# C11, the fourth and the sixth product: PSUM banks handed on by ScalarE's copies in place of VectorE's adds

## The chip, the cores and the metric

The kernel runs on one core of a Trainium2 chip. The metric is the time of an execution on the device in microseconds (us); the time of a kernel is the median of its runs.

## The reference

```
a, b: 4096 x 4096, float32, normally distributed; alpha = 0.01
x = a @ b
out = where(x > 0, x, alpha * x)        # float32
```

## The kernel before

The matrix product is done in 16-bit floats with 32-bit sums in PSUM, as a Strassen-Winograd scheme. The output is cut into 4 row groups `g` and 4 column groups `j` of 1024 each. The block (0, 0) is done plainly at the start (L283). The other 15 are "regions", done in the order (0,1) (0,2) (0,3), (1,2) (1,0) (1,3) (1,1), (2,2) (2,0) (2,3) (2,1), (3,2) (3,0) (3,1) (3,3).

A region's a and b are each cut into four blocks (A11 to A22, B11 to B22). Seven products take the place of eight; `product(n, ...)` (L808, its matmul at L819) does one as 64 matmuls, each of 128 x 128 weights on 128 x 512, into four PSUM banks. TensorE's order through a region is product 0 (A11 on B11), 1 (A12 on B21), 2, the fourth, 4, the sixth and the seventh; numbers count from 0 and ordinals from one, so "the fourth" is product 3. Some of these are cut once more in the same way: the fourth, the sixth and the seventh of most regions with g > 0, and the fifth of region (2,3) alone. Such a product is seven `quarter_product`s (L762) of 16 matmuls each, on 128 x 256.

The kinds of region: `first_of_group` (column 2), `turning` (the last of a group when the next group's A is loaded and transposed meanwhile: (0,3), (1,1), (2,1)), `in_quarters` (g > 0 and not turning), `in_fourth` (in_quarters and not the first of its group), `in_fifth` ((2,3)).

The eight PSUM banks are two sets of four, `y` and `z`; the sets change places from region to region. In the old kernel product 0 fills `y`, product 1 fills `z`, product 2 goes on in `y`, the fourth takes `z` again, product 4 goes on in `y`, the sixth takes `z`. What leaves the banks goes by two engines:

- ScalarE: `keep` (L829) copies four banks to tiles `c` in SBUF (L832), and the copies inside the quartered products.
- VectorE: `add` (L1041) adds four banks to tiles of SBUF, one instruction to each; in the quartered products it adds single banks (`more` in the sixth, the loop over `parts` for the fourth at L1219).

VectorE forms as well the sums of B's blocks (`b_sum`, L592) and of their quarters (L686 to L696, called `t3_of_b`, `sums_of_b`), the sums of A's, the leaky product at the end (L313), and the transposes of A. Quarter sums of A that come again (`kept_qs`, `kept_qa`) are stored in DRAM and loaded back (`load_sums`, L754).

Two things run beside the products and are ordered by hand. Measures (`measure(i, half, nt)`, begin and end) have ScalarE square a block of b (L231) and VectorE reduce the squares (L240 to L264); `EARLY` says which stand behind product 0 of which region (for (2,0): B12 and then B21), and `late_ones`, `middle` name other places. ScalarE also squares the rows of a (L611).

Loads: b comes through GpSimd's queue, which converts to 16 bit (`fetch_unit`, L536: pieces of 512 KB, two to a tile, so a pair of issues is one tile). `fetch_b(i + 1, ...)` puts the next region's tiles where tiles of the same block are now, so each pair waits for the last matmul that reads the tile it overwrites. In region (2,0) the four pairs for (2,3) are, in order, two that overwrite the block of B that the fourth reads and two that overwrite the block that product 4 reads; the last two are what product 0 of (2,3) reads. SyncE issues the stores of the output (L1054) and other loads; ScalarE issues a few.

The whole order is a schedule written out by hand (`manual_schedule`): each engine does its instructions in the order of the program.

Of the kernel before, what the change touches and what calls it, by code (L numbers as in the profile page):

```python
# [31 lines left out]
MT = 4  # L32
# [16 lines left out]
def kernel(  # L49
# [17 lines left out]
    nc = tc.nc  # L67
# [725 lines left out]
    for i, (g, j) in enumerate(regions):  # L793
# [14 lines left out]
        def product(n, banks, first):  # L808
            name, half, nt = PRODUCTS[n]

            ks_here = (0, 1) if n == 0 and second_of_group else ks
            todo = [(k, c) for k in ks_here for c in range(KC)]
            order = [(mt, k, c) for k, c in todo for mt in range(MT)]
            if n == 0 and late_s2:

                order = [(mt, k, c) for k in ks_here for mts in ((0, 1), (2, 3)) for c in range(KC) for mt in mts]
            for mt, k, c in order:
                t = operand(g, name, k)
                nc.tensor.matmul(  # L819
                    banks[mt], a_cols(t, c, mt, t is first_a), B(half, nt, k)[:, c, :],  # L820
                    start=first and (k, c) == todo[0], stop=(k, c) == todo[-1], skip_group_check=not first,
                )
# [12 lines left out]
        def fourth_in_quarters(banks, tq, sx):  # L835
# [11 lines left out]
            if not turning:  # L847
                quarter_product(sx[4], b[1, 1], into(other), True)
# [7 lines left out]
            if turning:  # L856
                quarter_product(sx[4], b[1, 1], into(other), True)
            return pairs, kept, [(block(r, n), pair(bank)) for r, n, bank in (
                (0, 0, fourth), (0, 1, other), (0, 1, third), (1, 0, one), (1, 1, one))]

# [43 lines left out]
        def sixth_in_quarters(pairs, banks, v_pairs, v, y, tq, sq, between=None):  # L904
# [4 lines left out]
            one, other, third, fourth = banks  # L909
# [13 lines left out]
            quarter_product(x[0, 0], b[0, 0], into(one), True)  # L923
            add(v[:2], y[:2])
            more(0, 0, one)
            add(v[2:], y[2:])
            quarter_product(sx(1), t(1), into(other), True)
            more(1, 1, other)
            following(4)
            next_t[2] = tq[1]  # L930
            quarter_product(x[0, 1], b[1, 0], into(fourth), True)
            if between:
                next(between)
            else:
                leave(v_pairs, 1, 1)
            quarter_product(sx(2), t(2), into(one))
            following(2)
            more(0, 1, one)
            if between:

                leave(v_pairs, 1, 1, (0,))
                t3_of_b(y7)
            sums_of_b(y7, next_t, (2,))
            more(0, 0, fourth)
            quarter_product(sx(4), b[1, 1], into(other))
            following(1, sq.get("room"))
            next_t[4] = tq[2]
            more_t4 = lambda: sums_of_b(y7, next_t, (4,))
            if not between:
                more_t4()  # L950
            more(0, 1, other)
            quarter_product(sx(3), b[0, 1], into(one))
            following(3, sq.get("last"))
            more(1, 0, one)
            more(1, 1, one)
            quarter_product(x[1, 1], t(4), into(third), True)
            if between:
                more_t4()
            more(1, 0, third)
# [153 lines left out]
        for n, m in enumerate(early):  # L1113
            if n:
                m.begin()
            m.end()
        have_t2 = g > 1 and j == CACHED
# [4 lines left out]
        u1_pairs, u1 = keep(y, side)  # L1122
# [12 lines left out]
        if middle:  # L1135
            middle.end()
        if g == 1 and j in OTHERS:
            keep_half()
# [7 lines left out]
        product(1, z, True)  # L1146
# [5 lines left out]
        add(u1, z)  # L1152
# [3 lines left out]
        if in_fourth:  # L1156
            tq = {n: new_a16() for n in (2, 4)}
            sx4 = new_a16()
            if not second_of_group:
                nc.sync.dma_start(sx4, kept_s3)  # L1160
            t3_of_b(quarters_of_b(i, 0, 1))
            sums_of_b(quarters_of_b(i, 0, 1), tq, (2,))
            if second_of_group:
                sums_of_s3(g, (4,), sx4)
            sums_of_b(quarters_of_b(i, 0, 1), tq, (4,))
# [21 lines left out]
        if in_fourth:  # L1187
            tq[1] = t[:, 3]
            sums_of_b(quarters_of_b(i, 0, 1), tq, (1,))
            b_sum(B(1, 0, ks[1]), B(1, 0, ks[1]), B(0, 0, ks[1]), SUB)  # L1190
        elif turning and g:
            tq, sx4 = {2: t[:, 0], 4: t[:, 1], 1: t[:, 2]}, t[:, 3]
            sums_of_b(quarters_of_b(i, 0, 1), tq, (2, 4, 1))
            nc.sync.dma_start(sx4, kept_s3)
# [16 lines left out]
        if in_fourth or turning and g:  # L1211
            v_pairs, v, parts = fourth_in_quarters(z, tq, {**s3_rooms(g), 4: a_quarter(sx4)})
            if turning:
                for n in range(3):
                    turn_a_in(0, 1, n)
            for n, (to, bank) in enumerate(parts):
                if in_fifth and n == 2:
                    sums_of_b(quarters_of_b(i, 0, 0), t5, (1,))
                nc.vector.tensor_add(to, bank, to)  # L1219
                if in_fifth and n == 0:  # L1220

                    t3_of_b(quarters_of_b(i, 0, 0))
                    sums_of_b(quarters_of_b(i, 0, 0), t5, (2, 4))
            if turning or in_fifth:
                add_v()
        else:
# [84 lines left out]
        if not in_quarters:  # L1311
            product(5, z, g > 0)
            add(u2[::-1], z[::-1])
# [115 lines left out]
```

## Time and profile before

| | us |
|---|---|
| median of the runs | 1532.78 (1531.96 to 1533.01, 3 runs) |
| profiled execution, span of core 0 | 1531.4 |
| TensorE matmuls, busy | 1521.0 (99%) |
| VectorE, busy | 1171.2 (76%) |
| ScalarE, busy | 428.1 (28%) |
| GpSimd, busy | 258.2 (17%) |
| granted TensorE clock | 1.00 |

For the profiled execution itself the span, 1531.4 us from its first to its last instruction, is all that is given; no run's time is marked as its own. In its lines L12 is line 12 of the kernel; engines are PE (TensorE's matmuls), PEld (its weight loads), DVE (VectorE), ACT (ScalarE), POOL (GpSimd), SP (SyncE). A group's line says line, engine, operation, output<-input with shape and type, x count, then busy us and mean ns of one, then the idle time before it and what ended it. A line of the timeline has start, duration, engine, line, operation, and in brackets the idle time ahead with its releaser.

### The profile page before, as it was taken

The page shows a single profiled execution, that of the slowest core. Times are in us where ns is not written, and L with a number is a line of the kernel's source. Part 1 is how long each engine was busy: PE and PEld are TensorE (multiplying, and loading weights), DVE is VectorE, ACT ScalarE, POOL GpSimd, SP SyncE. Part 2 cuts the span into 40 slices and gives each one's busy share as a digit, 9 for nine tenths or more (in the row PEclk, how much of TensorE's full clock was granted, in tenths as well). Part 3 has the DMA queues.
Part 4 walks back from the last instruction along what each step waited for, and adds up shares of the span by engine and source line. Part 5 has one row for each costly group of instructions (what it writes and reads, how often), then busy time and mean ns, then how long its engine had stood idle before and what let it go on. Part 6 is the DMA issues. An engine that isn't in the chain of part 4 may idle for free. (4 is left out here: it accounts for less than half of the span.)

```text
span 1531.4 us, 21934 instructions
## 1 busy us (share of the span) xinstructions
PE 1521.0 (99%) x8715; PEld 851.5 (56%) x8715; DVE 1171.2 (76%) x1231; ACT 428.1 (28%) x734; POOL 258.2 (17%) x426
## 2 busy tenths in 40 slices
PE   9999999999999999999999999999999999999998
PEld 4444444444446567574544747577544475746656
DVE  4378867766897676768789599688978868687677
ACT  2201334646310213103651130313464103041210
POOL 5641110143202011022220001000331100101000
PEclk9999999999999999999999999999999999999999
DMA  9999995998979999899898939859999892948824
GB/s 248 188 216 200 239 281 168 180 193 176 251 312 257 277 237 276 243 290 246 184 310 279 302 149 231 294 154 343 217 241 297 229 347 70 295 161 189 302 97 140
DMA packets 194258, 356.50 MB, mean 233 GB/s; under 512 B 18913, under 2 KB 132833, under 8 KB 181090
## 3 DMA queue, kind: packets, MB, share of 16 engines
q0 software_dynamic: 119808, 112.22, 46.4%
q1 hardware_dynamic: 67714, 217.22, 38.0%
q10 hardware_dynamic: 6624, 25.56, 4.4%
q8 instruction: 70, 1.15, 0.3%
q14 instruction: 42, 0.34, 0.1%
HBM read 347.61 MB, written 117.44 MB: 304 GB/s over the span
## 5 line engine op out<-in xcount | busy, mean ns | idle before, releaser
L819 PE MATMUL ps<-b,a 128*128 128x512 f16 x2624 | 570.7, 379 | 1.4 <-DMA b<-in_b_dram 1.4
L819 PE MATMUL ps<-b,s 128*128 128x512 f16 x2176 | 475.2, 379 | 0.0
L819 PEld LDWEIGHTS <-a 128*128 128x128 f16 x2624 | 256.7, 98 | 309.3 <-issue 1.7
L819 PEld LDWEIGHTS <-s 128*128 128x128 f16 x2176 | 212.8, 98 | 255.2 <-issue 0.4
L592 DVE TENSOR_TENSOR b<-b 128x4096 f16<-128x4096 f16 x104 | 234.8, 2286 | 46.0 <-DMA b<-in_b_dram 34.1
L536 POOL DMA_DIRECT2D b<-in_b_dram x128 | 94.8, 745 | 879.8 <-PE ps L762 448.2
L832 ACT COPY c<-ps 128x512 f32<-128x512 f32 x164 | 85.0, 596 | 483.2 <-PE ps L819 439.2
L142 DVE STREAM_TRANSPOSE a<-a 128x512 uint32<-128x512 uint32 (+2 forms) x120 | 127.0, 1105 | 78.9 <-DMA a<-in_a_dram 78.9
L133 POOL DMA_DIRECT2D a<-in_a_dram x252 | 137.4, 553 | 245.5 <-ACT junk L611 73.6
L762 PEld LDWEIGHTS <-q 128*128 128x128 f16 x1488 | 145.6, 98 | 16.9
L313 DVE SCALAR_TENSOR_TENSOR c<-c 128x1024 f32<-128x1024 f32 (+2 forms) x123 | 141.8, 1194 | 4.1 <-ACT c L832 3.8
L611 ACT ACTIVATE junk<-a 128x512 bf16<-128x512 f16 x192 | 121.1, 631 | 83.4 <-DMA a<-in_a_dram 78.1
L1041 DVE TENSOR_TENSOR c<-ps,c 128x512 f32<-128x512 f32 x140 | 87.5, 683 | 62.8 <-PE ps L819 51.2
L231 ACT ACTIVATE sq<-b 128x2048 bf16<-128x2048 f16 x64 | 118.4, 1910 | 38.8 <-DVE sq L240 31.0
L762 PEld LDWEIGHTS <-a 128*128 128x128 f16 x1200 | 117.4, 98 | 17.4
L283 PE MATMUL ps<-b,a 128*128 128x512 f16 x512 | 112.2, 379 | 0.5 <-ACT a L380 0.2
L762 PE MATMUL ps<-b,q 128*128 128x256 f16 x816 | 95.6, 273 | 0.0
L762 PE MATMUL ps<-b,a 128*128 128x256 f16 x752 | 88.3, 273 | 0.0
L283 PEld LDWEIGHTS <-a 128*128 128x128 f16 x512 | 49.7, 98 | 60.8 <-issue 1.4
L977 ACT COPY c<-ps 128x512 f32<-128x512 f32 x9 | 5.3, 586 | 255.6 <-PE ps L762 145.8
L762 PEld LDWEIGHTS <-s 128*128 128x128 f16 x672 | 65.7, 98 | 7.6
L762 PE MATMUL ps<-q,q 128*128 128x256 f16 x544 | 64.6, 273 | 0.0
(108 smaller groups left out, 917.0 us busy)
## 6 DMA issues: line engine op xcount, KB each, us to landing
b<-in_b_dram POOLq DMA_DIRECT2D x136, 512.0 KB, 11.8
out_dram<-c SPq DMA_DIRECT2D x240, 256.0 KB, 7.0
a<-in_a_dram POOLq DMA_DIRECT2D x244, 128.0 KB, 5.7
b<-kept_half SPq DMA_DIRECT2D x28, 1024.0 KB, 11.8
b<-kept SPq DMA_DIRECT2D x20, 1024.0 KB, 8.8
q<-kept_qs ACTq DMA_DIRECT2D x40, 512.0 KB, 7.8
s<-kept_s SPq DMA_DIRECT2D x18, 1024.0 KB, 7.6
q<-kept_qa SPq DMA_DIRECT2D x28, 512.0 KB, 7.5
```

What stands on the lines that cost most here:

```text
L133: nc.gpsimd.dma_start(a16[32 * q:32 * q + 32], src.rearrange("(g i) w -> i g w", i=32))
L142: nc.vector.transpose(part.rearrange("p c m e -> p c (m e)").bitcast(U32) .rearrange("p c (g i) -> p g c i", i=32), src[:, :, i * n:(i + 1 ...
L231: nc.scalar.activation(to, self.parts[n], SQUARE)
L283: nc.tensor.matmul(ps, a_cols(at[0, h, u], c, mt, (h, u) == (0, 0)), bt[0, u, nt][:, c, :], start=first, stop=last,)
L313: nc.vector.scalar_tensor_tensor(t, t, alpha, t, op0=MULT, op1=MAX if alpha <= 1 else MIN)
L536: nc.gpsimd.dma_start(t[:, c:c + 4, :], b_rows(j, u, c, 4, nt, g > 0))
L592: nc.vector.tensor_tensor(f(to), f(x0), f(x1), op)
L611: nc.scalar.activation(junk, piece[:, q, :], SQUARE, accum_out=to[:, 4 * n + q:4 * n + q + 1])
L762: nc.tensor.matmul(to[m], xq[:, c // 2, rows, c % 2], yq[:, c, :], start=first and c == 0 and m < banks, stop=c == KC - 1, skip_group_chec ...
L819: nc.tensor.matmul(banks[mt], a_cols(t, c, mt, t is first_a), B(half, nt, k)[:, c, :], start=first and (k, c) == todo[0], stop=(k, c) == t ...
L832: nc.scalar.copy(kept[mt], banks[mt])
L1041: nc.vector.tensor_add(to, bank, to)
```

## The change

In product 0 and 1 of every region: the last sixteen matmuls of product 0 and the first sixteen of product 1 go bank by bank. Behind product 0 and the first early measure ScalarE copies `y[mt]` to `z[mt]` for four banks; product 1 accumulates on `z`, and `keep(z)` takes the place of `keep(y)` and four adds. The second early measure (B21, in region (2,0) and (3,1)) begins behind these copies and ends behind the sums of B.

In the fourth of `in_fourth` regions a new function `fourth_by_seeds`, with a new order of the seven quarter products: a bank that holds a partial sum is copied by ScalarE to a second one, on which the next quarter product accumulates. Two adds of VectorE are left of five. The sums of b's quarters are made in the order 2, 1 and then 4. In the sixth likewise, with six adds in place of eight; two of the loads that follow are exchanged (`following`). In the turning regions product 5 accumulates on copies of `u2`, ScalarE copies the result back; the fourth's order there is one order for both cases.

```diff
--- before.py
+++ after.py
@@ -811,6 +811,10 @@
             ks_here = (0, 1) if n == 0 and second_of_group else ks
             todo = [(k, c) for k in ks_here for c in range(KC)]
             order = [(mt, k, c) for k, c in todo for mt in range(MT)]
+            if n == 0:
+                order[-16:] = [(mt, k, c) for mt in range(MT) for k, c in todo[-4:]]
+            elif n == 1:
+                order[:16] = [(mt, k, c) for mt in range(MT) for k, c in todo[:4]]
             if n == 0 and late_s2:
 
                 order = [(mt, k, c) for k in ks_here for mts in ((0, 1), (2, 3)) for c in range(KC) for mt in mts]
@@ -844,8 +848,6 @@
             quarter_product(x[0, 1], b[1, 0], into(fourth), True)
             quarter_product(x[0, 0], b[0, 0], into(one), True)
             nc.scalar.copy(block(0, 0), pair(one))
-            if not turning:
-                quarter_product(sx[4], b[1, 1], into(other), True)
             quarter_product(x[1, 1], t(4), into(third), True)
             nc.scalar.copy(block(1, 0), pair(third))
             quarter_product(sx[2], t(2), into(one))
@@ -853,10 +855,33 @@
             quarter_product(sx[1], t(1), into(third), True)
             nc.scalar.copy(block(1, 1), pair(third))
             quarter_product(sx[3], b[0, 1], into(one))
-            if turning:
-                quarter_product(sx[4], b[1, 1], into(other), True)
+            quarter_product(sx[4], b[1, 1], into(other), True)
             return pairs, kept, [(block(r, n), pair(bank)) for r, n, bank in (
                 (0, 0, fourth), (0, 1, other), (0, 1, third), (1, 0, one), (1, 1, one))]
+
+        def fourth_by_seeds(banks, tq, sx):
+
+            pairs, kept = new_c(side)
+            b = quarters_of_b(i, 0, 1)
+            x = quarters_of_a(g, "s3")
+            chain, shared, one, other = banks
+            t = lambda n: b_quarter(tq[n])
+            block = lambda r, n: pairs[r][:, :, n * HALF:(n + 1) * HALF]
+            quarter_product(x[0, 0], b[0, 0], into(chain), True)
+            nc.scalar.copy(one, chain)
+            quarter_product(sx[1], t(1), into(shared), True)
+            quarter_product(sx[2], t(2), into(chain))
+            nc.scalar.copy(other, chain)
+            quarter_product(x[0, 1], b[1, 0], into(one))
+            nc.scalar.copy(block(0, 0), pair(one))
+            quarter_product(sx[3], b[0, 1], into(chain))
+            nc.scalar.copy(one, chain)
+            nc.scalar.copy(block(1, 1), pair(chain))
+            quarter_product(sx[4], b[1, 1], into(other))
+            nc.scalar.copy(block(0, 1), pair(other))
+            quarter_product(x[1, 1], t(4), into(one))
+            nc.scalar.copy(block(1, 0), pair(one))
+            return pairs, kept, [(block(r, 1), pair(shared)) for r in (1, 0)]
 
         def fifth_in_quarters(y, one, other, tq, sq, between):
 
@@ -906,7 +931,7 @@
 
             b = quarters_of_b(i, 1, 0)
             x = quarters_of_a(g, "a22")
-            one, other, third, fourth = banks
+            chain, shared, one, other = banks
             t = lambda n: b_quarter(tq[n])
             sx = lambda n: a_quarter(sq[n])
             next_t, next_s = {}, {}
@@ -920,43 +945,40 @@
                 next_s[n] = new_a16() if room is None else room
                 load_sums("s4", next_s, (n,), nc.scalar)
 
-            quarter_product(x[0, 0], b[0, 0], into(one), True)
-            add(v[:2], y[:2])
-            more(0, 0, one)
-            add(v[2:], y[2:])
-            quarter_product(sx(1), t(1), into(other), True)
-            more(1, 1, other)
+            quarter_product(x[0, 0], b[0, 0], into(chain), True)
+            nc.scalar.copy(one, chain)
+            add(v, y)
+            quarter_product(sx(1), t(1), into(shared), True)
             following(4)
             next_t[2] = tq[1]
-            quarter_product(x[0, 1], b[1, 0], into(fourth), True)
             if between:
                 next(between)
+                leave(v_pairs, 1, 1, (0,))
+                t3_of_b(y7)
             else:
                 leave(v_pairs, 1, 1)
-            quarter_product(sx(2), t(2), into(one))
+            quarter_product(sx(2), t(2), into(chain))
+            nc.scalar.copy(other, chain)
             following(2)
-            more(0, 1, one)
+            sums_of_b(y7, next_t, (2,))
+            quarter_product(x[0, 1], b[1, 0], into(one))
+            more(0, 0, one)
+            next_t[4] = tq[2]
+            if not between:
+                sums_of_b(y7, next_t, (4,))
+            for r in (0, 1):
+                more(r, 1, shared)
+            quarter_product(sx(3), b[0, 1], into(chain))
+            nc.scalar.copy(one, chain)
+            more(1, 1, chain)
+            following(1, sq.get("last"))
+            quarter_product(sx(4), b[1, 1], into(other))
             if between:
-
-                leave(v_pairs, 1, 1, (0,))
-                t3_of_b(y7)
-            sums_of_b(y7, next_t, (2,))
-            more(0, 0, fourth)
-            quarter_product(sx(4), b[1, 1], into(other))
-            following(1, sq.get("room"))
-            next_t[4] = tq[2]
-            more_t4 = lambda: sums_of_b(y7, next_t, (4,))
-            if not between:
-                more_t4()
+                sums_of_b(y7, next_t, (4,))
             more(0, 1, other)
-            quarter_product(sx(3), b[0, 1], into(one))
-            following(3, sq.get("last"))
+            following(3, sq.get("room"))
+            quarter_product(x[1, 1], t(4), into(one))
             more(1, 0, one)
-            more(1, 1, one)
-            quarter_product(x[1, 1], t(4), into(third), True)
-            if between:
-                more_t4()
-            more(1, 0, third)
             next_t[1] = tq[4]
             sums_of_b(y7, next_t, (1,))
             if between:
@@ -1110,16 +1132,17 @@
         product(0, y, True)
         if second_of_group:
             sums_of_s3(g, (2,))
-        for n, m in enumerate(early):
-            if n:
-                m.begin()
+        for m in early[:1]:
             m.end()
+        for mt in range(MT):
+            nc.scalar.copy(z[mt], y[mt])
+        for m in early[1:]:
+            m.begin()
         have_t2 = g > 1 and j == CACHED
         if have_t2:
             for k in ks:
                 t = have_b[i, k, 0] = b_pool.tile([P, KC, NT], DT, name="b", tag="b11")
                 move_t("t2", t, k, False, nc.scalar)
-        u1_pairs, u1 = keep(y, side)
         if middle:
             middle.begin()
         for k in ks:
@@ -1134,6 +1157,8 @@
                 move_t("t2", B(0, 0, k), k, True)
         if middle:
             middle.end()
+        for m in early[1:]:
+            m.end()
         if g == 1 and j in OTHERS:
             keep_half()
         note_rows()
@@ -1143,18 +1168,18 @@
                 sum_a(g, "s4")
         bring_a(0, 0, range(1 if g else 4))
 
-        product(1, z, True)
+        product(1, z, False)
         if turning and g:
 
             b_sum(B(1, 0, ks[0]), B(1, 0, ks[0]), B(0, 0, ks[0]), SUB)
             t3_of_b(quarters_of_b(i, 0, 1))
             bring_a(0, 0, [1, 2])
-        add(u1, z)
+        u1_pairs, _ = keep(z, side)
         leave(u1_pairs, 0, 0)
         if g:
             bring_a(0, 0, [3])
         if in_fourth:
-            tq = {n: new_a16() for n in (2, 4)}
+            tq = {n: new_a16() for n in (2, 1)}
             sx4 = new_a16()
             if not second_of_group:
                 nc.sync.dma_start(sx4, kept_s3)
@@ -1162,7 +1187,7 @@
             sums_of_b(quarters_of_b(i, 0, 1), tq, (2,))
             if second_of_group:
                 sums_of_s3(g, (4,), sx4)
-            sums_of_b(quarters_of_b(i, 0, 1), tq, (4,))
+            sums_of_b(quarters_of_b(i, 0, 1), tq, (1,))
         if (g, j) == (0, LAST):
             keep_half()
         if i == 0:
@@ -1185,8 +1210,8 @@
         if g:
             t = x_pool.tile([P, 4, QUARTER], DT, name="q", tag="x")
         if in_fourth:
-            tq[1] = t[:, 3]
-            sums_of_b(quarters_of_b(i, 0, 1), tq, (1,))
+            tq[4] = t[:, 3]
+            sums_of_b(quarters_of_b(i, 0, 1), tq, (4,))
             b_sum(B(1, 0, ks[1]), B(1, 0, ks[1]), B(0, 0, ks[1]), SUB)
         elif turning and g:
             tq, sx4 = {2: t[:, 0], 4: t[:, 1], 1: t[:, 2]}, t[:, 3]
@@ -1209,20 +1234,23 @@
 
         z = [new_bank(zbank + mt) for mt in range(MT)]
         if in_fourth or turning and g:
-            v_pairs, v, parts = fourth_in_quarters(z, tq, {**s3_rooms(g), 4: a_quarter(sx4)})
+            fourth = fourth_by_seeds if in_fourth else fourth_in_quarters
+            v_pairs, v, parts = fourth(z, tq, {**s3_rooms(g), 4: a_quarter(sx4)})
             if turning:
                 for n in range(3):
                     turn_a_in(0, 1, n)
+            if in_fifth:
+
+                t3_of_b(quarters_of_b(i, 0, 0))
+                sums_of_b(quarters_of_b(i, 0, 0), t5, (2, 4, 1))
             for n, (to, bank) in enumerate(parts):
-                if in_fifth and n == 2:
-                    sums_of_b(quarters_of_b(i, 0, 0), t5, (1,))
                 nc.vector.tensor_add(to, bank, to)
-                if in_fifth and n == 0:
-
-                    t3_of_b(quarters_of_b(i, 0, 0))
-                    sums_of_b(quarters_of_b(i, 0, 0), t5, (2, 4))
             if turning or in_fifth:
                 add_v()
+            if turning:
+                z = [new_bank(zbank + mt) for mt in range(MT)]
+                for mt in range(MT):
+                    nc.scalar.copy(z[mt], u2[mt])
         else:
             product(3, z, True)
             v_pairs, v = keep(z, side)
@@ -1309,8 +1337,12 @@
         fetch_b(i + 1, [(0, 0)], (1, 0) if in_fifth else ks)
 
         if not in_quarters:
-            product(5, z, g > 0)
-            add(u2[::-1], z[::-1])
+            product(5, z, False)
+            if g:
+                for mt in range(MT):
+                    nc.scalar.copy(u2[mt], z[mt])
+            else:
+                add(u2[::-1], z[::-1])
         if turning:
 
             bring_a(1, 1, range(3))
```

## The prediction

> **What bounds the kernel now.** I began with the page's busy shares and its costliest lines.
>
> ```profile
> span 1531.4 us, 21934 instructions
> ...
> PE 1521.0 (99%) x8715; PEld 851.5 (56%) x8715; DVE 1171.2 (76%) x1231; ACT 428.1 (28%) x734; POOL 258.2 (17%) x426
> ...
> L819 PE MATMUL ps<-b,a 128*128 128x512 f16 x2624 | 570.7, 379 | 1.4 <-DMA b<-in_b_dram 1.4
> ```
>
> TensorE is busy for 1521.0 of 1531.4 us. The change leaves the number of matmuls as it is and only re-orders some, so what VectorE sheds is worth nothing as busy time: only a wait of TensorE's can be shortened. The second view is therefore all of TensorE's waits, each with its total, count and longest.
>
> ```profile
> PE ps L819 <- DMA b<-in_b_dram: 1.4, 1, 1.4
> PE wp L106 <- DVE x L92: 1.2, 1, 1.2
> PE turned L373 <- DVE a_rounded L357: 1.1, 1, 1.1
> PE ps L283 <- ACT a L380: 0.2, 1, 0.2
> ```
>
> Together 3.9 us. The last three belong to the start, which the change does not touch. The one in reach is 1.4 us: once, a matmul of `product` waits for a tile of b. The third view, the chain of waits, gives its place and what releases it.
>
> ```profile
> 945.38 33.41 DMA b<-in_b_dram
> 978.79 0.04 issue
> 978.84 32.97 PE ps L819 x152
> ```
>
> A piece of b issued at 945.38 lands 33.41 us later, and from there on the chain is TensorE alone. So the most that can be gained is about 1.4 us, 0.1%. The question is what the new orders make late. About 0.2% (3.1 us) is what a measurement of this kernel can tell from no change.
>
> The profiled span, 1531.4 us, is 1.4 us below the median of the runs, 1532.78; I add changes of the span to the median.
>
> **Handing on banks in the first two products.** Product 1's four VectorE adds go, four ScalarE copies PSUM to PSUM come. The rows nearest to them:
>
> ```profile
> L1041 DVE TENSOR_TENSOR c<-ps,c 128x512 f32<-128x512 f32 x140 | 87.5, 683 | 62.8 <-PE ps L819 51.2
> L832 ACT COPY c<-ps 128x512 f32<-128x512 f32 x164 | 85.0, 596 | 483.2 <-PE ps L819 439.2
> ...
> 545.10 2.06 ACT L832 COPY c<-ps 128x512 f32<-128x512 f32 x4 [26.12 <-PE ps L819]
> 876.60 27.79 PE L819 MATMUL ps<-b,a 128*128 128x512 f16 x128
> ```
>
> Four copies in a row take 2.06 us, 0.5 each. Products 0 and 1 run on without a gap: 128 matmuls in 27.79 us, 0.217 each. The diff orders the last sixteen of product 0 and the first sixteen of product 1 bank by bank, four matmuls or 0.87 us to a bank. Hence the first bank is ready 3 × 0.87 = 2.6 us ahead of product 1, and copies that follow 0.5 us apart keep ahead of matmuls that want a bank every 0.87 us. No trace row shows a copy from PSUM into PSUM. From below it is bounded by nothing faster than 0.5 us, from above by the add of two such operands, 0.68; both are under 0.87, so I put the wait at nothing, if ScalarE is free. It works in order, so what stands before the copies matters. The tightest place is region (3,2), where squares of a's rows are queued:
>
> ```profile
> 1155.68 27.79 PE L819 MATMUL ps<-b,a 128*128 128x512 f16 x128
> ...
> 1167.12 0.63 ACT L611 ACTIVATE junk<-a 128x512 bf16<-128x512 f16 x1
> ```
>
> Product 1 begins at 1155.68 + 64 × 0.217 = 1169.6; the last square ends at 1167.75. Copies from then on end at 1168.3, 1168.8 and so on: 1.3 us to spare. In region (2,0) the squares of b21 are moved behind the copies, and so take nothing from them:
>
> ```profile
> 888.27 5.51 ACT L231 ACTIVATE sq<-b 128x2048 bf16<-128x2048 f16 x3 [1.29 <-DVE sq L243]
> ```
>
> They were queued at 888.27 and ended at 893.78, while product 1 starts at 890.4; the new place is what makes the copies possible. Queued behind the copies on ScalarE are these squares (VectorE's part of the measure comes later, beside product 1) and the loads of the second sums; each has over ten us before its reader. The turning regions seed product 5 in the same way, in a hole of ScalarE's:
>
> ```profile
> 1125.69 0.63 ACT L611 ACTIVATE junk<-a 128x512 bf16<-128x512 f16 x1 [5.24 <-DMA a<-in_a_dram]
> 1128.06 2.32 PE L819 MATMUL ps<-b,a 128*128 128x512 f16 x10
> ```
>
> ScalarE idles 5.24 us ahead of 1125.69 and product 5 starts at 1128.06: room for 2.1 us of copies. All of this: 0. In the fourth and sixth a copy of one bank has the quarter product between (1.75 us by the starts below), about three times its 0.6 us: 0.
>
> **The fourth in a new order.** Here lies the main term. The two tiles of b that the fourth reads come free behind their last readers: in the old order behind the third quarter product (`sx[4]` on b11) and the seventh (`sx[3]` on b01), in the new one behind the fifth (`sx[3]` on b01) and the sixth (`sx[4]` on b11). GpSimd's fetches of the next region's b go into tiles that come free. Region (2,0), TensorE and then GpSimd:
>
> ```profile
> 918.15 3.66 PE L762 MATMUL ps<-b,a 128*128 128x256 f16 x32
> ...
> 923.39 1.91 PE L762 MATMUL ps<-q,a 128*128 128x256 f16 x16
> 925.14 1.91 PE L762 MATMUL ps<-q,s 128*128 128x256 f16 x16
> 926.88 1.91 PE L762 MATMUL ps<-q,a 128*128 128x256 f16 x16
> ...
> 924.09 1.48 POOL L536 DMA_DIRECT2D b<-in_b_dram  x2 [70.00 <-PE ps L762]
> 931.08 1.48 POOL L536 DMA_DIRECT2D b<-in_b_dram  x2 [5.52 <-PE ps L762]
> 937.75 1.48 POOL L536 DMA_DIRECT2D b<-in_b_dram  x2 [5.18 <-PE ps L819]
> 944.65 1.48 POOL L536 DMA_DIRECT2D b<-in_b_dram  x2 [5.43 <-PE ps L819]
> ```
>
> The first pair goes out behind the third quarter product. Two products later is 926.88 − 923.39 = 3.5 us, so it goes out at about 927.6; the second pair comes one product, 1.75 us, earlier, at 929.3. The last two pairs wait for product 4, which stays. These eight pieces are the ones of which the last stalls TensorE at 977. What did the DMA engines do before and in that time (us; busy PE, PEld, DVE, ACT, POOL; granted clock; DMA share; GB/s)?
>
> ```profile
> 920.00:925.00 5.00, 5.00 (x48) 4.49 (x46) 5.00 (x4) 0.59 (x1) 0.91 (x2) 1.00 0.00 0
> 925.00:930.00 5.00, 5.00 (x48) 4.47 (x47) 4.97 (x4) 1.76 (x3) 0.56 (x1) 1.00 1.03 160
> 970.00:975.00 5.00, 5.00 (x25) 2.29 (x24) 5.00 (x8) 5.00 (x3) 0.00 (x0) 1.00 1.13 328
> ```
>
> Until 925 they idle, from then on they are full (share 1.03, and 1.13 still at 970). So 3.5 us of a full queue system are lost at its start, when the fetch had it alone. How much later does the last piece land? The first and the last pair, from issue to landing (minimum, median, maximum):
>
> ```profile
> DMA to landing us min/median/max: 5.2/6.5/7.9
> ...
> DMA to landing us min/median/max: 27.3/30.4/33.4
> ```
>
> With issues 0.74 us apart, the first pair lands 7.9 + 0.74 − 5.2 = 3.4 us apart, a piece's price alone; the last pair 33.4 + 0.74 − 27.3 = 6.8 us apart, a piece's price beside the stores and loads of SyncE and ScalarE: factor 2.0. Over all six later pieces it is (978.8 − 932.7)/6 = 7.7 us, factor 2.25. Work of 3.4 us of a lone queue costs 6.8 us where the others press on, so the last piece is late by 3.5 × 2.0 = **7.0 us**; bounds 0 (others yield, their work being done later) and 3.5 × 2.25 = 7.9. I take 7.0 as the last pair is the one that decides. Its lateness falls on TensorE in full, since the stall is there already. By the Trainium skill's page "DMA: Bandwidth & Descriptors", section "Queues, rings and completion order", each engine serves the queue rows that hold work in turn, packet by packet; with a third row busy too that would be a factor 3 and 10.5 us. The rows show 2.0 to 2.25, and I go by them.
>
> **The sixth in a new order.** In region (2,3) the fourth sum of A is fetched late:
>
> ```profile
> L754 SPq DMA_DIRECT2D q<-kept_qa x1: 320/320/320, 1036.3 to 1036.3; - x1
> DMA to landing us min/median/max: 7.8/7.8/7.8
> ...
> 1041.33 1.91 PE L762 MATMUL ps<-q,q 128*128 128x256 f16 x16
> 1043.08 3.66 PE L762 MATMUL ps<-b,q 128*128 128x256 f16 x32
> ```
>
> It is issued at 1036.29, when the fifth's last reader has left its tile, and lands at 1044.1. The product that reads it (`sx(3)`) was the sixth, at 1044.83, and becomes the fifth, at 1043.08: **1.0 us** of wait; 0 to 2, as the landing shifts. With less other traffic it could land in time.
>
> VectorE has fewer adds in the fourth and sixth (three and two of 0.68 us), off the path; a hole of 0.1 us at 904, where its second sum was late behind b21's measure, may go: −0.1.
>
> The sum: 1532.8 + 7.0 + 1.0 − 0.1 = **1540.7 us**.
>
> **Rivals.** *B, the late fetch is absorbed.* SyncE's and ScalarE's transfers could wait instead, or the pair that goes out 1.75 us sooner make up for it. Then only the sixth's 1.0 us remains: 1532.8 + 1.0 − 0.1 = 1533.7, no change. For it: the second pair is sooner; against it: it stands in the same queue behind the first pair.
>
> *C, the other side.* VectorE's load slows GpSimd's fetch, and with the adds gone the fetch runs faster from the same start. At 925 to 930 VectorE is busy 4.97 of 5 us and 160 GB/s flow; where it was less busy:
>
> ```profile
> 570.00:575.00 5.00, 5.00 (x41) 3.75 (x39) 2.75 (x5) 0.00 (x0) 1.48 (x2) 1.00 1.10 174
> ```
>
> That is 9% more with VectorE at 2.75. Eight pieces of 3.4 us, 9% quicker, save 2.4 us; the decision is whether that exceeds the delay of the pair, which must then be under 1.0 us for the stall to vanish. Then 1532.8 − 1.4 − 0.1 = 1531.3: not slower. The skill's page "SBUF — State Buffer", section "Who interferes with whom", speaks against it: sums of two tensors have no mode that takes GpSimd's write port.
>
> *D, ScalarE is late at the seeds.* If a copy from PSUM to PSUM took 1.0 us instead of 0.5, each bank would come 0.13 us later than wanted: some 0.4 us in each of 15 regions, 6 us, on top of A: 1546.7. It decides from 0.87 us a bank on. Nothing in the rows is that slow (0.68).
>
> **How the numbers follow.** A, the fetch late: 0.57, its own range 1536 to 1545. B 0.25, C 0.10, D 0.08. The predicted time is A's, 1540.7. The range runs from 1533.0 (B with 0.3 us of the sixth's wait) to 1545.0 (A with 7.9 and 2.0, 1542.6, and a third of D); it leaves out C, D and a rest. Slower by over 0.2%, above 1535.8: A and D, 0.65. Within: B, most of C, 0.33. Faster by over 0.2%: 0.02, since the waits in reach hold 1.4 us.
>
> **What would show it.** In the profile after: GpSimd's pair at 927 to 928 instead of 924.09, the last piece's landing at 984 to 987, and TensorE's wait for b at `product`'s line at 7 to 9 us in place of 1.4; a wait of 1 us for kept sums of A in the sixth of (2,3); no wait of TensorE's for ScalarE. It is wrong if the pair goes out as before, or if the last piece lands before 981, or if the wait lies on ScalarE's copies.

## The result, and the profile after

| | before | after |
|---|---|---|
| median of four runs of each, us | 1532.59 (1531.96 to 1533.01) | 1544.02 (1543.25 to 1544.35) |
| ratio | | 1.0064 (1.005 to 1.0079) |
| span of the profiled execution, us | 1531.4 | 1541.9 (this execution's time: 1544.03) |

The kernel became 11.4 us slower; 1540.7 was predicted, 1533.0 to 1545.0 as the range. The page after, with the lines that answer to those of before, and TensorE's waits:

```profile
span 1541.9 us, 21982 instructions
...
PE 1523.6 (99%) x8715; PEld 852.0 (55%) x8715; DVE 1107.5 (72%) x1122; ACT 496.0 (32%) x861; POOL 258.1 (17%) x426
...
L823 PE MATMUL ps<-b,a 128*128 128x512 f16 x2624 | 573.0, 380 | 9.9 <-DMA b<-in_b_dram 9.9
```

```profile
PE ps L823 <- DMA b<-in_b_dram: 9.9, 3, 7.4
PE wp L106 <- DVE x L92: 1.2, 1, 1.2
PE turned L373 <- DVE a_rounded L357: 0.8, 1, 0.8
PE ps L762 <- DVE q L694: 0.7, 1, 0.7
PE ps L283 <- ACT a L380: 0.2, 1, 0.2
```

VectorE shed 63.7 us (1171.2 to 1107.5) and ScalarE took 67.9 (428.1 to 496.0), and neither shows in the time. None of the waits listed in the body of the kernel is for ScalarE; one of 0.29 us, too short for this list, comes below under the sixth. The wait for b at the matmul of `product` (now L823) went from 1.4 us to 9.9, in three waits that all lie in product 0 of (2,3). The chain says which piece:

```profile
945.21 42.28 DMA b<-in_b_dram
987.54 34.85 PE ps L823 x152
```

It is the same last piece, out at the same moment (945.38 before) and landing at 987.5 instead of 978.8. GpSimd's issues, and TensorE's granted clock behind the wait (the columns of the prediction's windows):

```profile
927.41 2.99 POOL L536 DMA_DIRECT2D b<-in_b_dram  x4 [73.38 <-PE ps L762]
937.58 1.48 POOL L536 DMA_DIRECT2D b<-in_b_dram  x2 [7.18 <-PE ps L823]
944.48 1.48 POOL L536 DMA_DIRECT2D b<-in_b_dram  x2 [5.43 <-PE ps L823]
```

```profile
985.00:990.00 5.00, 2.46 (x6) 0.84 (x6) 3.59 (x2) 0.00 (x0) 0.00 (x0) 0.50 0.95 374
990.00:995.00 5.00, 5.00 (x21) 2.14 (x20) 0.20 (x1) 1.47 (x3) 0.00 (x0) 0.86 0.04 13
```

The first two pairs now go out one behind the other from 927.41 on. Behind the wait of 7.4 us the granted clock is 0.50: eight matmuls start 0.427 us apart instead of 0.217.

Laying the starts of the products of both traces beside each other gives where the time went (differences that arise in a product, us):

```
product 0 of (2,3)              +10.76   (13.81 without any wait; before 15.37, after 26.13)
fourth of (2,1)                  +0.89
sixth of (2,3)                   +0.29
product 1 of (2,0)               -0.11
all others together              below 0.1
start of the last seventh        +11.73
```

The 26.13 us of product 0 are 13.81 + 10.36 (the last piece lands that much after its matmul would start) + 1.96 for the half clock. The span grew by less than 11.73, by 10.5 us, because the time from the start of the last matmul to the end of the span is 5.3 us in this trace and 6.5 before; it takes 5.3 to 6.8 us over all traces, with the change and without, so this part is scatter.

### The profile page after: what moved, and what is told of

It reads as the page before. It is cut to its first block, busy times and chain, and to the rows that moved or that the text cites. A ratio compares the mean times of both kernels' runs of the same rounds, so it can differ in the third digit from the quotient of the medians.

```text
span 1541.9 us, 21982 instructions
## 1 busy us (share of the span) xinstructions
PE 1523.6 (99%) x8715; PEld 852.0 (55%) x8715; DVE 1107.5 (72%) x1122; ACT 496.0 (32%) x861; POOL 258.1 (17%) x426
## 4 chain that ended last, share of the span: by engine, by line
PE 92%; DMA 6%; DVE 1%; ACT 0%; issue 0%; SPq 0%; POOL 0%; ACTq 0%; POOLq 0%; DVEq 0%
PE ps L823 64%; PE ps L762 21%; PE ps L283 7%; DMA b<-in_b_dram 3%; DMA a<-in_a_dram 1%; DMA s<-kept_s 1%; DMA b<-kept_half 1%; DMA a_in<-in_a_dram 0%; ACT junk L611 0%; DVE c L1063 0%; DVE q L694 0%; DVE q L692 0%; DVE c L313 0%; DVE b L592 0%; DVE a L142 0%
## 5 line engine op out<-in xcount | busy, mean ns | idle before, releaser
L823 PE MATMUL ps<-b,a 128*128 128x512 f16 x2624 | 573.0, 380 | 9.9 <-DMA b<-in_b_dram 9.9
L823 PE MATMUL ps<-b,s 128*128 128x512 f16 x2176 | 475.2, 379 | 0.0
L823 PEld LDWEIGHTS <-a 128*128 128x128 f16 x2624 | 257.2, 98 | 319.5 <-issue 13.3
L823 PEld LDWEIGHTS <-s 128*128 128x128 f16 x2176 | 212.8, 98 | 255.1
L836 ACT COPY c<-ps 128x512 f32<-128x512 f32 x164 | 84.0, 599 | 289.8 <-PE ps L823 289.8
L1063 DVE TENSOR_TENSOR c<-ps,c 128x512 f32<-128x512 f32 x72 | 44.6, 683 | 73.1 <-PE ps L823 73.1
L1138 ACT COPY ps<-ps 128x512 f32<-128x512 f32 x60 | 32.8, 572 | 172.2 <-PE ps L823 172.2
L762 PE MATMUL ps<-q,q 128*128 128x256 f16 x640 | 73.5, 273 | 0.0
```

The source lines that it names most:

```text
L762: nc.tensor.matmul(to[m], xq[:, c // 2, rows, c % 2], yq[:, c, :], start=first and c == 0 and m < banks, stop=c == KC - 1, skip_group_chec ...
L823: nc.tensor.matmul(banks[mt], a_cols(t, c, mt, t is first_a), B(half, nt, k)[:, c, :], start=first and (k, c) == todo[0], stop=(k, c) == t ...
L836: nc.scalar.copy(kept[mt], banks[mt])
```

## The experiments

The theory under test: the fetch of the next region's b is late because the DMA engines stand idle longer ahead of it. The rivals: the copies on the banks; the stores of SyncE that come sooner; the bare start of the first pair.

**Undo the fourth where it hurts.** In region (2,0) alone the old order, adds and order of sums.

```diff
-            fourth = fourth_by_seeds if in_fourth else fourth_in_quarters
+            by_seeds = in_fourth and (g, j) != (2, 0)
+            fourth = fourth_by_seeds if by_seeds else lambda *x: fourth_in_quarters(*x, in_fourth)
...
-            tq = {n: new_a16() for n in (2, 1)}
+            soon, late = (4, 1) if (g, j) == (2, 0) else (1, 4)
+            tq = {n: new_a16() for n in (2, soon)}
```

> The changed kernel with the old fourth (order, adds, order of the sums of b) in region (2,0) alone; all else is changed. Theory (the late fetch): the first pair of pieces of b goes out near 924 again, the last one lands near 979, TensorE waits about 1.5 us at product 0 of (2,3), and the 10.8 us that this product lost come back: 1533.3 us, with the 0.9 us of region (2,1) left. Rival (the copies in product 1, or VectorE being sooner with its sums and so SyncE with its stores): the last piece lands at 983 or later and the time stays above 1537.

Measured: 1534.3 us, ratio to before 1.0005 (0.9995 to 1.0014). TensorE's waits in the body:

```profile
PE ps L762 <- DVE q L694: 1.1, 1, 1.1
PE ps L823 <- DMA b<-in_b_dram: 0.9, 1, 0.9
```

All other copies stand, and the loss is gone: it sits in the fourth of one region of fifteen.

**The fetch late, and nothing else.** The kernel before, one quarter product moved in (2,0).

```diff
-            if not turning:
+            here = (g, j) == (2, 0)
+            if not turning and not here:
                 quarter_product(sx[4], b[1, 1], into(other), True)
...
             quarter_product(sx[2], t(2), into(one))
             nc.scalar.copy(block(0, 1), pair(one))
+            if here:
+                quarter_product(sx[4], b[1, 1], into(other), True)
```

> The kernel before, with one quarter product of region (2,0) moved: sx[4] on b11 fifth instead of third. Nothing else moves. Theory: the first pair goes out 3.5 us later, at 927.5, the second as before at 931.1; the last piece lands 7 to 9 us later, 986 to 988, and with slow matmuls behind the wait the time is 1540.5 to 1543.5. Rival (the stores that came 2 us sooner in the changed kernel, not the fetch's start, made the difference): last landing before 982, time under 1536.

Measured: 1544.05 us, 1.0068 (1.0051 to 1.0085). The wait, GpSimd's issues, and the time from issue to landing of the last pair (the maximum is the last piece, issued at 945.71):

```profile
PE ps L819 <- DMA b<-in_b_dram: 8.7, 1, 8.7
```

```profile
927.90 1.48 POOL L536 DMA_DIRECT2D b<-in_b_dram  x2 [73.49 <-PE ps L762]
931.41 1.48 POOL L536 DMA_DIRECT2D b<-in_b_dram  x2 [2.02 <-PE ps L762]
```

```profile
DMA to landing us min/median/max: 31.7/36.8/41.8
```

With no copy of the change in it this kernel is as slow as the changed one, and the last piece lands as late: 945.7 + 41.8 = 987.5. Product 0 of (2,3) took 9.5 us longer than before (10.76 in the changed kernel). That the two times agree to 0.1 us is chance: here another 1.1 us came in the sixth of (2,0), where an add of VectorE's was late (VectorE had waited 3.6 us for stores of SyncE's to land, 1.7 before), and 1.4 us in the fourth of (2,1). Those 1.1 and 1.4 us put the time above the range expected.

**Half the delay.** The same, with the quarter product fourth.

```diff
             nc.scalar.copy(block(1, 0), pair(third))
+            if here:
+                quarter_product(sx[4], b[1, 1], into(other), True)
             quarter_product(sx[2], t(2), into(one))
```

> The kernel before with sx[4] on b11 fourth instead of third in region (2,0): the fetch's first pair goes out 1.75 us later, at 925.9, the stores as before at 929.2. Theory: the engines start 1.75 us later, the last piece lands 5.2 us later, at 984; TensorE waits some 6 us at product 0 of (2,3) and runs some matmuls at half clock behind it: 1538 to 1541. By the factor 2.0 of the prediction it would land at 982.3 and the time be 1536.

Measured: 1539.2 us, 1.0043 (1.0031 to 1.0055). The profiled execution was the shortest of its six:

```profile
PE ps L819 <- DMA b<-in_b_dram: 3.3, 1, 3.3
```

```profile
980.00:990.00 10.00, 7.36 (x35) 3.35 (x35) 9.75 (x12) 2.15 (x4) 0.00 (x0) 1.00 1.02 406
```

The last piece landed 62.6 us after the fourth began, against 60.6 before: 1.9 us for 1.75 us of delay in this one trace, not the 5.2 that the theory expected. The time is in its range, but in this trace product 0 of (2,3) lost only 1.9 us against before and the fourth of (2,1) another 1.3, so the range was not met for the theory's reason. Behind a wait of 3.3 us the clock stays at 1.00. Spans of the five other executions were 1.2 to 2.3 us longer, four of them at a mean clock of 0.998; only this one was traced.

**The stores first.** The changed kernel; VectorE's sums of S1's quarters go ahead of two sums of B, and SyncE's stores of them with them.

```diff
+        s1_sums = {}
+        if s1_here:
+            sums_of_a(g, "s1", lambda n: t[:, n - 1], (1, 2, 3), s1_sums)
         for k in ks:
             b_sum(B(0, 0, k), B(1, 1, k), B(0, 0, k), SUB)
         if late_ones:
             late_ones[0].end()
-        s1_sums = {}
-        if s1_here:
-            sums_of_a(g, "s1", lambda n: t[:, n - 1], (1, 2, 3), s1_sums)
```

> The changed kernel with VectorE's three sums of S1's quarters in region (2,0), and so their stores, put ahead of two sums of B: the stores go out 4 us sooner, while the DMA engines idle. Theory (what is lost is time in which the fetch has the DMA engines to itself): the last piece lands near 983, 4 us sooner than in the changed kernel, time near 1539. Rival (only the start of the pair counts): the pair goes out at 927.4 as in the changed kernel and the last piece lands at 987.5; time 1544.

Measured: 1532.6 us, 0.9995 (0.9986 to 1.0005). TensorE's waits, all of them; GpSimd's first issues; and the last piece's landing:

```profile
PE wp L106 <- DVE x L92: 1.2, 1, 1.2
PE turned L373 <- DVE a_rounded L357: 0.9, 1, 0.9
PE ps L283 <- ACT a L380: 0.2, 1, 0.2
```

```profile
927.91 2.99 POOL L536 DMA_DIRECT2D b<-in_b_dram  x4 [73.38 <-PE ps L762]
```

```profile
DMA to landing us min/median/max: 24.8/27.1/29.3
```

The pair goes out as late as in the changed kernel, and the last piece lands 13.0 us sooner reckoned from the fourth's begin. The late pair was harmless here, with the DMA engines at work meanwhile: three stores of 512 KB were out 4.4 us sooner. The gain is three times what the theory gave.

**Both on the kernel before: the fetch late, the stores first.**

> The kernel before with both edits: sx[4] on b11 fifth in region (2,0), so the fetch's first pair goes out near 927.7, and the three stores put ahead of the two sums of B, near 924 to 927. Theory (idle time of the DMA engines is what costs): they start at 924, the last piece lands at 975 to 980 in spite of the late pair, time 1532 to 1535. Rival (the start of the pair, as the prediction had it): landing at 986 to 988 and 1541 to 1544, as when the pair alone was late.

Measured: 1532.7 us, 0.9998 (0.9988 to 1.0007).

```profile
928.20 1.48 POOL L536 DMA_DIRECT2D b<-in_b_dram  x2 [73.48 <-PE ps L762]
```

```profile
925.36 2.72 SPq L710 DMA_DIRECT2D kept_qs<-q  x3
```

```profile
DMA to landing us min/median/max: 25.5/27.8/30.1
```

This differs from the second experiment in the stores alone (929.47 there). The same late pair, and 946.0 + 30.1 = 976.1 instead of 987.5. That the start of the pair decides by itself, as the prediction had it, is refuted.

**The stores first on the kernel before.**

> The kernel before, with VectorE's three sums of S1's quarters in region (2,0), and their stores, ahead of the two sums of B: stores go out at about 924 to 927, beside the fetch's first pair at 924.1. Theory (the last piece lands 3 us later for each us that the DMA engines stand idle ahead of it: 975.0 for a start at 923.3, 978.6 for 924.35, 987.5 for 927.2): they start at 924, so the last piece lands at 977 to 979, the wait at product 0 of (2,3) is 0 to 1.5 us, and the time within 1.5 us of before. Rival (stores ahead of the fetch are good in themselves): landing at 975 or sooner. Rival (the fetch must have its first pair alone): landing at 982 or later, time above 1536.

Measured: 1533.0 us, 0.9998 (0.9988 to 1.0008); no wait for b, last landing at 977.2 (57.6 us after the fourth's begin).

**The stores late.** The changed kernel; the three stores stand behind SyncE's first load of a kept sum.

```diff
-            load_sums("a22", sq, order)
+            load_sums("a22", sq, order[:1])
+            while held_stores:
+                nc.sync.dma_start(*held_stores.pop(0))
+            load_sums("a22", sq, order[1:])
```

> The changed kernel with those three stores issued behind SyncE's first load of a kept sum, at about 933 to 935 instead of 927.2 to 929.6; the sums stay where they are. Theory: the first pair has the DMA engines to itself for 5 us as in the kernel before, its first piece lands 5 to 6 us after its issue instead of 7.9, the last one near 983; time near 1539. Rival (only the total of bytes ahead of the last piece counts): last landing within 1 us of 987.5, time 1543 to 1545.

Measured: 1538.9 us, 1.004 (1.0026 to 1.0054).

```profile
PE ps L767 <- DVE q L696: 4.4, 1, 4.4
PE ps L767 <- DMA q<-kept_qa: 1.3, 1, 1.3
```

The time is what the theory expected, but not for its reason: the sums that overwrite the stored tiles now wait for the stores, TensorE waits 4.4 us for them and then runs at half clock for a while, 6.2 us in all, and the transfers behind shift with it: SyncE's next stores of the output go out at 957.41 instead of 948.61. The wait for b is gone (landing at 977.2), though the pair went out as late as in the changed kernel and the DMA engines idled as long ahead of it. The run doesn't separate the theory from its rival, but it shows that the idling alone does not fix the landing: what the other queues move beside the fetch counts too.

**The banks of products 0 and 1 alone.** The kernel before with that part of the change.

> The kernel before with the first part of the change alone: order of products 0 and 1 by banks, ScalarE's copies of y to z, product 1 on them, keep(z) for keep(y) and four adds, the second early measure behind the copies. Fourth, sixth and the turning regions' product 5 as before. Theory: nothing at the copies, fetch as before, landing near 979, time within 1.5 us of before; in the turning region (2,1) 0 to 1.4 us of wait for a quarter sum of b if the copies behind ScalarE's squares cause that. Rival (ScalarE late at the seeds): waits of product 1 for ScalarE, time above 1536.

Measured: 1532.0 us, 0.9988 (0.9978 to 0.9998). No wait for a copy, and none for b; in the turning region (2,1):

```profile
PE ps L762 <- DVE q L694: 0.8, 1, 0.8
```

```profile
1095.78 2.36 DVE L313 SCALAR_TENSOR_TENSOR c<-c 128x1024 f32<-128x1024 f32 x2 [2.63 <-ACT c L836]
```

VectorE's leaky step waits for ScalarE's copies `keep(z)`, which stand behind the squares of a's rows.

**Each kernel once more,** for the scatter of a single profile.

> The kernel before once more, for the scatter of a single profile. The last piece lands 60.6 us after the fourth of (2,0) begins in the first profile; here within 1.5 us of that, and TensorE waits 0 to 2 us at product 0 of (2,3) and 0 to 1 us in the fourth of (2,1).

> The changed kernel once more, for the same scatter: last landing within 1.5 us of 69.5 us after the fourth's begin, wait of 7 to 9 us at product 0 of (2,3) with half clock behind it, 0 to 1.5 us in the fourth of (2,1).

Measured, before: 1533.5 us, no wait for b at all, last landing 57.4 us after the fourth's begin (60.6 in the first profile: twice the scatter expected), but

```profile
PE ps L762 <- DVE q L694: 1.7, 1, 1.7
```

So the wait in (2,1) occurs in the old kernel too, in some executions. After: 1544.5 us, landing 69.0 us (69.5), a wait of 8.7 us for the last piece.

**Both mended:** the stores first, and in turning regions `keep(z)` right behind product 1, ahead of the squares.

```diff
         product(1, z, False)
+        if turning:
+            u1_pairs, _ = keep(z, side)
...
-        u1_pairs, _ = keep(z, side)
+        if not turning:
+            u1_pairs, _ = keep(z, side)
```

> The changed kernel with the three stores first, as in the run of that name, and with ScalarE's four copies keep(z) of the turning regions put ahead of the squares of a's rows. Theory: no wait at product 0 of (2,3); VectorE's leaky step in (2,1) no longer waits for those copies (2.2 to 2.6 us in the runs that have them), so the quarter sums of (2,1) are in time unless a's pieces land late: wait there 0 to 0.5 us; time 0.5 to 2 us under before. Rival (a's pieces alone decide the wait in (2,1)): 1 us or more there in spite of it.

Measured: 1531.5 us, 0.9987 (0.9978 to 0.9995) to before: the lowest median of all, though the 1532.0 us of the banks alone lie within the noise of it. The span is 1529.4 us, and these are all the waits:

```profile
PE wp L106 <- DVE x L92: 1.2, 1, 1.2
PE turned L373 <- DVE a_rounded L357: 0.2, 1, 0.2
```

VectorE's leaky step in (2,1) follows without a wait for ScalarE. Whether that is what spared the wait in the fourth there stays open: the stores-first run had none either, with the copies late.

All traces in one table, us from the begin of the fourth of (2,0). The last piece is due at 59.2 to 60.3, with the stores late some 6 us later:

```
run                         first pair out  first store out  last piece lands
changed, stores first            9.43            4.79             56.5
both mended                      9.43            4.79             57.3
before, late, stores first       9.43            6.59             57.3
before, stores first             5.94            6.60             57.6
before (two profiles)            5.94           11.0              60.6, 57.4
banks alone                      5.94            9.19             58.7
old fourth in (2,0)              5.94            9.20             60.2
changed, stores late             9.43           13.9              59.1
before, half late                7.69           11.0              62.6
before, fetch late               9.43           11.0              69.1
changed (two profiles)           9.43            9.20             69.5, 69.0
```

But for the run with the stores late, what orders the landings is the sooner of the two columns, the time at which the DMA engines get to work again: 4.8 to 6.6 gives 56.5 to 60.6, 7.7 gives 62.6, 9.2 and 9.4 give 69 to 69.5. The run with the stores late stands outside this order (9.4 and 59.1): there the transfers of the other queues were held up as well. From 5.94 (mean of the five: 58.9) to 9.2 it is 10.3 us for 3.3 us of longer idling, a factor near 3; it isn't a straight line, and each row but two rests on a single trace.

## Why the prediction was right, and what in it was not

**What bounds the kernel** stood: VectorE's 64 us less are worth nothing, and the wait at product 0 of (2,3) is where the time is decided.

**The copies at nothing** stood, but for the 0.29 us under the sixth below. A copy from PSUM into PSUM took 0.57 us, between the bounds of 0.5 and 0.68:

```profile
L1138 ACT COPY ps<-ps 128x512 f32<-128x512 f32 x60 | 32.8, 572 | 172.2 <-PE ps L823 172.2
```

ScalarE waits for TensorE there, not TensorE for ScalarE. Rival D is out. One reading was cut off by its window: of b21's squares in region (2,0) there are four, to 895.6, not three to 893.78. That only strengthens the argument for moving them.

**The fourth.** The pair went out at 927.41 (927.6 forecast), with the second pair behind it, and the wait grew where it was forecast; the landing (987.5) and the waits for b (9.9 us in all) lie a little beyond the signs that were named, 984 to 987 and 7 to 9 us. Mis-sized was the factor 2.0, "a piece's price beside the stores and loads", taken from the spacing of the last pair. Reckoned from the fourth's begin the pair went out 3.5 us later (5.94 to 9.43) and the last piece landed 8.9 us later (60.6 to 69.5), a factor of 2.5; between the second profiles (57.4 to 69.0) it is 11.6 us and 3.3. The share of the queues of SyncE, of b's fetch and of a third queue before, in the stretch that ends shortly ahead of product 0's wait, bears on it (packets, MB, share of the 16 engines):

```profile
q1 hardware_dynamic: 1355, 4.23, 56.6%
q0 software_dynamic: 1132, 1.12, 32.8%
q10 hardware_dynamic: 432, 1.57, 19.4%
```

Over 955 to 975 the fetch has a third of the engines, not half. It moved nearly as many packets as SyncE's queue, but packets of about 1 KB against about 3 KB. For a third busy queue the prediction had named a factor 3 and 10.5 us and set it aside; the 8.9 and 11.6 us lie on both sides of that. The same row of the fetch's queue for 925 to 955, before and after:

```profile
q0 software_dynamic: 3077, 3.07, 64.5%
```

```profile
q0 software_dynamic: 2429, 2.42, 51.0%
```

By 955 it is 0.65 MB behind, and at its rate of 955 to 975 (1.12 MB in 20 us before, 1.29 MB after) that takes 10 to 12 us to move. This is an estimate from two traces; no run varied the share, so why the factor is near 3 is argued and not shown. The spacing of the last two landings did not tell of it.

The step was also wrong in what it charged: the start of the pair. That start by itself cost nothing here: with the stores sent into the idle stretch the pair was as late and the loss was gone. What costs is a late pair behind idle DMA engines, with the other queues coming on as before. Nor did the prediction price the clock: the half clock behind the long wait, 1.96 us, is in none of its terms. In product 0, 10.36 us of lateness and 1.96 of clock, less the 1.56 that product 0 lost before, make the 10.76.

**The sixth.** The 1.0 us did not come. The load of `sx(3)` was issued at the forecast place and landed in 6.6 us instead of 7.8, 0.2 us before its product:

```profile
DMA to landing us min/median/max: 6.6/6.6/6.6
```

The 0.29 us that this sixth lost come from a copy of ScalarE's that had to wait for VectorE's add of the bank it writes; it ends at 1057.40, and the next quarter product starts at 1057.45. The sum had it at nothing:

```profile
1056.83 0.57 ACT L972 COPY ps<-ps 128x512 f32<-128x512 f32 x1 [4.09 <-DVE c L942]
```

So the low size of one term (7.0 for 8.9, plus 2.0 of clock) was partly made up by another that stayed away. That the measured 1544.0 us lie in the range is luck in part: A's own terms reach 1542.6 at most, and the range went up to 1545.0 only by a third of D, which did not occur. The hole at 904 went, −0.11, as forecast. The 0.89 us in (2,1) were not forecast; the kernel before shows 1.86 us there in its second profile, so they need not be the change's.

**Rivals B and C.** With the late fetch the other transfers did not yield. A fetch that is faster beside a less busy VectorE was not seen: with the banks alone the last piece lands at 58.7, against 60.6 and 57.4 before. B's remark that something sooner could make up for it was near the truth, with the stores in the part of the second pair.

## What to carry to other kernels

Where a late transfer stalls the engine that bounds the kernel, look back for the stretch in which the DMA engines were idle: a transfer that is ready can be put there, as the stores were here, and it need not be the one that is late. See first who waits for the tiles that such a transfer reads: stores sent later held up TensorE for 4.4 us. Price a delay at a shared queue by its share of the engines in the stretch before the deadline, not by the spacing of its last pieces. One order of quarter products decided 11 us out of 1530; the copies and adds that moved between two engines with time to spare decided 0.3 us.

## What had not been expected of the hardware

A wait of 7.4 to 8.7 us was followed by eight to twelve matmuls at half clock (0.427 us apart, granted clock 0.50), which cost 2.0 to 2.7 us more than the wait; behind 3.3 us there were none. The wait of 4.4 us with the stores late, which ended at 950.47, was followed by a slower clock too: from 950 to 955 the mean granted clock was 0.66. The Trainium skill's page "TensorE: Matmul & The Clock Gate", section "Part 1: The HAM clock gate", puts the drop to half rate after an idle window of about 3.4 us; the cases here lie on its two sides, 3.3 us without the drop and 4.4 us and more with it.

One profile of before showed the last piece of b landing 3.2 us later than another of the same kernel, and the wait of 1.4 us for it, from which the prediction began, is missing in the second. A stall of that size in a single profile is a draw.
